# Moving the final residual tasks and weight sums of a two-layer mixer kernel into one half of its second block, and reordering the first block's background tasks

## The chip, the cores and the metric

The kernel runs on one core of one Trainium2 chip. The metric is device time in microseconds (us), the median of several runs. Profiles are of one execution. The engines are named as in the profile: PE (TensorE, matmuls), PEld (its weight loads), DVE (VectorE), ACT (ScalarE), POOL (GpSimd) and SP (SyncE); SPq is SP's queue, from which most loads are issued, and POOL issues the stores.

## What is computed

Two layers over a residual stream x of 2048 tokens by 1024 channels, all in fp32:

```python
for l in range(DEPTH):                                   # 2 layers
    mod = silu(c) @ w_ada[l] + b_ada[l]                  # conditioning: shift, scale, gate
    shift, scale, gate = jnp.split(mod, 3, axis=-1)
    h = rms_norm(x, g_pre[l]) * (1.0 + scale) + shift
    proj = h @ w_in[l]                                   # 1024 -> 3072
    # u_a, b_a, c_a, gate_a, u_p, gate_p: 512 columns each
    y_a = b_a * causal_conv3(c_a * u_a, w_conv[l]) * silu(gate_a)
    y_p = pool(u_p, w_pool[l], pool_scale[l]) * silu(gate_p)
    y = jnp.concatenate([y_a, y_p], axis=-1) @ w_out[l]  # 1024 -> 1024
    x = x + gate * rms_norm(y, g_post[l])
```

`pool` takes causal means over 2, 4, 8 and 16 tokens, less the token itself, and mixes each group of 128 channels with a 128 x 128 matrix. Every fp32 matmul is made of three products of high and low parts.

## The kernel before

**Blocks.** There are four blocks: layer 0 tokens 0 to 1023, layer 0 tokens 1024 to 2047, then the same for layer 1. A block has an input stage (the product with `w_in`, with the convolution and pooling behind it) and an output stage (the product with `w_out`, `out_phase`), in which the operands of the next block's input stage are made as well. The first block's input stage is plain (`in_phase`): for a pair of 512-token halves, 24 groups of 128 columns, each 8 turns; a turn is one 128-channel slice, three passes over two halves, six matmuls (line 395, the same line as in the output stage). The third and fourth block multiply three groups of a kind at a time with seven products instead of eight (`in_seven`, line 868), from weight sums that were computed earlier and stored in DRAM (`sums`). The second block is mixed: its first twelve column groups are done plainly (`in_phase` with `some` given, 96 turns, here called the **plain half**), its last six pairs by `in_seven` (the **sevenths half**, 42 products of 12 matmuls, which makes its own sums from the raw weights on DVE, lines 758 to 765).

**Background tasks.** Work that belongs to other blocks is cut into tasks with a load part and a list of steps with an estimated cost in us. `Paced` runs them between the turns: it spreads the estimated total evenly over a given number of turns (in the plain half over 72 of its 96, so that all are done some 10 turns before its end), holds at most two tasks open (`abreast=2`), and asks for the load of the next task when a task is begun (`lead` 1). The order in which the code calls the engines is the order of each engine's queue (`manual_schedule`): a queue does nothing behind an instruction that waits. The tasks that matter here:

- `mix_task`: two parts of a layer-one pooling weight; loads `wupt` (line 415), four small PE matmuls (line 421), stores `wu`.
- fills (`fill` in `out_phase`): load `late` (line 1123), cast on ACT, subtract on DVE (line 1134); operands of the sevenths half.
- `finish_tasks`, the **final tasks**, 16 of them: load `ysp` (line 1180) and x (line 1181), DVE multiply (1184) and add (1186), POOL store to `x1` (1191), ACT square (1197), DVE sum (1200). After the eighth of each half `stat_steps` splits the sum on ACT and DVE (368, 370), and five turns later PE forms the mean (313).
- `sum_task`, the **weight sums** of layer one: four loads of 128 KB (456), four DVE operations (464 to 467), ACT casts (470, 472), DVE subtractions (474, 476), four POOL stores of 256 KB (478, 479, two at 481).
- `x_stat_task` and `x_stat_end`: squares of the first layer's x for the second block, and their mean.
- `ada_task`: conditioning, two loads and two DVE operations (263, 267) a task; 8 for layer zero's gate and 16 for layer one's scale and shift.

**Buffers.** Loads of tasks land in `landing` tiles of 128 x 512, four in the first block and five in the second; the build gives a new tile the buffer that the program freed first, and the load then waits for that buffer's last reader or store. In the second block a final task takes two, a sum two, a fill and a mix one each. The final task's second tile (x) is the one that is stored, so it is free when the store has landed; the first is free after the square's sum (line 1200). Sums in the first block land in wide tiles of another pool.

**Weights.** In the plain stages `Weights` loads a half of a column group (line 202, SP) 16 turns before PE uses it, casts it on ACT (211) and forms the low part on DVE (221) six turns before.

Of the kernel before, what the change touches and what calls it, by code (L numbers as in the profile page):

```python
# [16 lines left out]
KT = D // P  # L17
# [4 lines left out]
NH = TB // HS  # L22
# [11 lines left out]
def trunk(ctx: ExitStack, tc: tile.TileContext, xt, c, wada, vec, rcp, win, wupt, wpool, wout, out):  # L34
# [210 lines left out]
    def ada_fin(l, kind, k0, k1):  # L245
        s = slice(kind * KT + k0, kind * KT + k1)
        ks = slice(k0, k1)
        nc.vector.tensor_tensor(mod[:, l, s], mod[:, l, s], mod2[:, l, s], op=ALU.add)
        nc.vector.tensor_tensor(mod[:, l, s], mod[:, l, s], vecs[:, l, V_ADA + s.start : V_ADA + s.stop], op=ALU.add)
        if kind == 1:  # L250
            nc.vector.scalar_tensor_tensor(
                apre[:, l, ks], mod[:, l, s], 1.0, vecs[:, l, V_PRE + k0 : V_PRE + k1], op0=ALU.add, op1=ALU.mult
            )
        elif kind == 2:
            nc.vector.tensor_tensor(gg[:, l, ks], mod[:, l, s], vecs[:, l, V_POST + k0 : V_POST + k1], op=ALU.mult)

    def ada_task(l, j):
        w = []

        def load():  # L260
            for n in range(2):
                w.append(landing("adaw"))
                nc.sync.dma_start(w[n], wada[l, j][:, n * HS : (n + 1) * HS])

        def steps():
            for n, m in enumerate((mod, mod2)):
                nc.vector.scalar_tensor_tensor(  # L267
                    w[n], w[n], 1.0, cb[:, n * HS : (n + 1) * HS], op0=ALU.mult, op1=ALU.mult, accum_out=m[:, l, j : j + 1]
                )
                yield E2  # L270

        return load, steps, 2 * E2

    def call_task(f, us):
        def steps():
            f()
            yield us

        return (lambda: None), steps, us
# [1183 lines left out]
    def between(many, few):  # L1463

        r, n = [], len(few)
        for i, t in enumerate(many):
            r.append(t)
            r += few[i * n // len(many) : (i + 1) * n // len(many)]
        return r

    with working(9, 4, 4, 3, 0):
        with tc.manual_schedule(engines={E.DVE, E.PE, E.Activation}):
            hrhs, started = start(0)
        with tc.manual_schedule():
            later = Later()
            accs = {}
            tasks = [mix_task(0, g, n, later) for g in range(1, NCG) for n in range(2)]
            rest = [ada_task(0, 2 * KT + k) for k in range(KT)]
            rest += [call_task(lambda: ada_fin(0, 2, 0, KT), 0.3)]
            rest += [ada_task(1, j) for j in list(range(8, 16)) + list(range(8))]  # L1480
            rest += [call_task(lambda: (ada_fin(1, 1, 0, KT), ada_fin(1, 0, 0, KT)), 0.5)]
            rest += [x_stat_task(1, s, k, accs) for s in range(NH) for k in range(KT)]
            tasks += between(rest, [sum_task(1, n, u, True) for n, u in mine("AB")])
            tasks += [x_stat_end(1, s, accs, later) for s in range(NH)]
            tasks += [call_task(lambda: load_wpool(1), 0.1)]
            ws = out_weights(0, turned(wplaces, 34))
            y = in_phase(0, 0, hrhs, tasks, later, started, yplaces, wplaces, ws)
# [39 lines left out]
    with working(5, 6, 5, 6, 2), tc.manual_schedule():  # L1527
        plain = [(kind, i) for kind, i in IN_ORDER if i < PLAIN]
        pairs = [(kind, i) for kind, i in PAIRS if i >= PLAIN]
        first = in_weights(0, plain, 0, turned(ws.places, 16))  # L1530
        h, fills, opening, hrhs = out_phase(0, 0, y, 0, 1, ws, hplaces, yorder, first, True)
        ring = first.places + hplaces[8 : 8 + KH]
        wts = Sevenths(0, ring, pairs, True)
        later = Later()
        mixes = [mix_task(1, g, n, later) for g in range(NCG) for n in range(2)]
        fins = finish_tasks(0, 0, later)
        sums_ = [sum_task(1, n, u, False) for n, u in mine("P")]
        cut = 6
        tasks = between(fills, mixes) + between(fins[:cut], sums_[:3])
        in_phase(0, 1, hrhs, tasks, later, None, None, first.places, wts, first, opening, plain)  # L1540
        hp = {}
        for k in range(KH):
            hp["B11", k], hp["B21", k], hp["B22", k] = hplaces[k], hplaces[KH + k], hplaces[12 + k]
        it = iter(yorder)
        for name in ("T2", "T3", "T1", "T4"):
            for k in range(KH):
                hp[name, k] = next(it)
        ws, closing, done = block_end(0, 1, hp, ring, pairs, False, (3, 2, 3, 2, 2, 2))
        kept = in_seven(0, 1, h, [], None, between(fins[cut:], sums_[3:]), later, wts, closing, pairs)
        y, yorder, wplaces, hplaces, _ = done(kept)  # L1550
    with working(5, 8, 6, 3, 2), tc.manual_schedule():
        for n, (l, b) in enumerate(blocks[2:], 2):
            lplaces = yorder[4:]
            ring = wplaces[1:] + yorder[:4] + wplaces[:1]
            wts = Sevenths(l, ring, PAIRS)
# [62 lines left out]
```

## Time and profile before

| | us |
|---|---|
| median of 3 runs | 1437.48 (1436.09 to 1438.05) |
| the profiled execution | 1435.26, span 1433.5 |
| PE busy | 1379.6 (96%), 6178 matmuls |
| DVE busy | 982.8 (69%) |
| ACT / POOL busy | 522.6 / 227.0 |
| DMA | 306.97 MB, mean 214 GB/s |

The profile gives busy time by engine, by group of instructions (line, engine, operation, tiles, count, mean duration, idle time before it and what ended it), the chain of work that ended last, who waited for whom, and a timeline. Times of instructions are us from the span's start. PE is busy 96% of the span, so what can be won or lost lies in the few stretches where it isn't dense.

### The profile page before, as it was taken

Reading aid. Unit: us, or ns where it says so; the run is one execution under the profiler, and the core shown is the slowest. Engines: PE = TensorE matmul, PEld = TensorE weight load, DVE = VectorE, ACT = ScalarE, POOL = GpSimd, SP = SyncE. Lnnn points to the kernel's source line nnn. Section 1 sums busy time; section 2 is a strip of 40 time slices with the busy share of each in tenths; the row PEclk is TensorE's granted clock in tenths of the full one; section 3 lists DMA queues with packets and bytes.
Section 4 is the critical chain, followed back from the end, with each engine's and each line's share of the span. In section 5 each row is a group of like instructions: output and inputs, shape, how many; then the busy total and the mean of one; then the engine's idle time right before and its main releaser. Section 6 shows DMA issues by size and latency. Waiting matters only on the chain.

```text
span 1433.5 us, 17996 instructions
## 1 busy us (share of the span) xinstructions
PE 1379.6 (96%) x6178; PEld 1126.0 (79%) x6178; DVE 982.8 (69%) x1645; ACT 522.6 (36%) x905; POOL 227.0 (16%) x365
## 2 busy tenths in 40 slices
PE   8999999989999999796999999999999999999996
PEld 4778888878888888565688888888888888888796
DVE  7765988956645568688775767768766755657555
ACT  5332324445643323232755321213656211112421
POOL 0001213211100111111022121221112122221000
PEclk9999999999999999998999999999999999999998
DMA  8416888855627563455567888797559777877422
GB/s 318 176 45 224 282 308 289 299 191 175 236 91 239 186 219 125 177 169 187 183 238 256 265 264 251 228 284 238 194 201 302 211 237 229 255 224 239 154 89 88
DMA packets 149598, 306.97 MB, mean 214 GB/s; under 512 B 16641, under 2 KB 33025, under 8 KB 149506
## 3 DMA queue, kind: packets, MB, share of 16 engines
q1 hardware_dynamic: 100658, 179.44, 38.2%
q0 software_dynamic: 48848, 126.38, 26.3%
q8 instruction: 48, 0.79, 0.2%
q14 instruction: 44, 0.36, 0.1%
HBM read 225.54 MB, written 80.22 MB: 213 GB/s over the span
## 4 chain that ended last, share of the span: by engine, by line
PE 73%; issue 9%; DVE 9%; DMA 5%; ACT 2%; POOL 1%; SPq 1%; DVEq 0%; ACTq 0%; POOLq 0%
PE ps_in L868 31%; PE ps_out L395 23%; PE ps_in L395 17%; DMA raw<-win 1%; PE ps_wu L421 1%; DMA sums<-raw 1%; DMA raw<-wout 1%; DVE y L188 1%; DVE ws L221 1%; DVE win L497 1%; DMA fin<-xt 0%; PE ps_warm L1304 0%; DVE adaw L267 0%; PE ps_stat L1321 0%; DMA xin<-xt 0%
## 5 line engine op out<-in xcount | busy, mean ns | idle before, releaser
L868 PE MATMUL ps_in<-h,ws 128*128 128x512 f32 x2520 | 583.8, 392 | 24.1 <-ACT ws L777 13.2
L868 PEld LDWEIGHTS ps_in<-h,ws 128*128 128x128 f32 x2520 | 473.5, 189 | 133.0 <-ACT ws L777 16.9
L395 PE MATMUL ps_out<-y,ws 128*128 128x512 f32 (+1 forms) x1728 | 355.6, 367 | 5.1 <-ACT ws L211 2.1
L395 PEld LDWEIGHTS ps_out<-y,ws 128*128 128x128 f32 x1728 | 298.0, 189 | 62.2 <-ACT ws L211 3.9
L395 PE MATMUL ps_in<-h,ws 128*128 128x512 f32 x1392 | 321.3, 391 | 0.0
L395 PEld LDWEIGHTS ps_in<-h,ws 128*128 128x128 f32 x1392 | 261.4, 189 | 54.1
L211 ACT CAST ws<-raw 128x512 fp32r<-128x512 f32 x122 | 74.7, 621 | 192.2 <-PE ps_in L395 73.0
L221 DVE TENSOR_TENSOR ws<-raw,ws 128x512 fp32r<-128x512 f32 x122 | 83.2, 687 | 83.2 <-ACT ws L211 83.2
L777 ACT CAST ws<-raw 128x512 fp32r<-128x512 f32 x108 | 65.3, 618 | 170.7 <-DMA raw<-win 49.0
L740 POOL DMA_DIRECT2D ws<-sums x96 | 67.6, 705 | 207.4 <-PE ps_in L868 178.7
L395 PE MATMUL ps_in<-h,w 128*128 128x512 f32 x336 | 81.1, 400 | 5.6 <-DVE h L387 2.8
L395 PEld LDWEIGHTS ps_in<-h,w 128*128 128x128 f32 x336 | 63.2, 190 | 22.6 <-DVE h L387 3.6
L787 DVE TENSOR_TENSOR ws<-raw,ws 128x512 fp32r<-128x512 f32 x108 | 73.9, 685 | 7.3 <-ACT ws L777 7.1
L1067 POOL DMA_DIRECT2D ysp<-yg x48 | 26.1, 545 | 217.6 <-ACT yg L1066 217.0
L267 DVE SCALAR_TENSOR_TENSOR adaw<-adaw,cb 128x512 f32<-128x512 f32 x64 | 42.5, 686 | 15.6 <-PE ps_wu L421 9.2
L912 ACT ACTIVATE second<-second 128x1024 f32<-128x1024 f32 x20 | 21.2, 1062 | 85.5 <-DVE second L906 82.6
L891 ACT COPY v<-ps_in 128x512 f32<-128x512 f32 x30 | 17.6, 585 | 83.2 <-PE ps_in L868 83.2
L1186 DVE TENSOR_TENSOR fin<-fin 128x512 f32<-128x512 f32 x48 | 32.9, 685 | 20.1 <-DMA fin<-xt 20.0
L1075 DVE TENSOR_TENSOR acc<-acc,sq 128x512 f32<-128x512 f32 x42 | 28.6, 690 | 21.2 <-ACT sq L1072 21.1
L906 DVE TENSOR_TENSOR second<-ps_in,v 128x512 f32<-128x512 f32 x20 | 13.8, 688 | 41.3 <-PE ps_in L868 41.3
L1066 ACT ACTIVATE yg<-ps_out,gg 128x512 f32<-128x512 f32 x48 | 33.0, 689 | 14.7 <-PE ps_out L395 14.7
L478 POOL DMA_DIRECT2D sums<-s13h x24 | 17.3, 719 | 129.6 <-ACT s13h L470 108.1
(191 smaller groups left out, 1341.4 us busy)
## 6 DMA issues: line engine op xcount, KB each, us to landing
ws<-sums POOLq DMA_DIRECT2D x96, 512.0 KB, 7.3
raw<-win SPq DMA_DIRECT2D x122, 256.0 KB, 4.9
adaw<-wada SPq DMA_DIRECT2D x64, 256.0 KB, 4.9
raw<-wout SPq DMA_DIRECT2D x64, 256.0 KB, 4.7
sums<-raw POOLq DMA_DIRECT2D x48, 256.0 KB, 4.9
ysp<-yg POOLq DMA_DIRECT2D x48, 256.0 KB, 3.5
fin<-ysp SPq DMA_DIRECT2D x48, 256.0 KB, 5.0
yraw<-yin SPq DMA_DIRECT2D x42, 256.0 KB, 4.1
```

Source lines behind the costliest of these rows:

```text
L211: nc.scalar.copy(self.ws[m][:, 0], self.raws[m].rearrange("p (a b) -> p a b", b=P))
L221: nc.vector.tensor_tensor(t[:, 1], raw, t[:, 0].bitcast(F32), op=ALU.subtract)
L267: nc.vector.scalar_tensor_tensor(w[n], w[n], 1.0, cb[:, n * HS : (n + 1) * HS], op0=ALU.mult, op1=ALU.mult, accum_out=m[:, l, j : j + 1])
L395: nc.tensor.matmul(ps[s], lhsT=ws[k // KH][:, wi, k % KH, :], rhs=rhs(k, ri, s), start=first and (wi, ri) == PASSES[0], stop=last and (wi, ...
L740: nc.gpsimd.dma_start(t.rearrange("p a b c -> p a (b c)"), sums[self.l, PAIRS.index((kind, i))][:, :, SUM[a]])
L777: nc.scalar.copy(self.place(m)[:, 0], self.raws[m].rearrange("p (a b) -> p a b", b=P))
L787: nc.vector.tensor_tensor(t[:, 1], raw, t[:, 0].bitcast(F32), op=ALU.subtract)
L868: nc.tensor.matmul(ps, lhsT=ops[m][:, wi, k, :], rhs=h[hn][k][:, ri, :], start=p < 4 and k == 0 and (wi, ri) == (0, 0), stop=k == KH - 1 a ...
L1066: nc.scalar.activation(t, ps[s], AF.Copy, scale=gg[:, l, j : j + 1])
L1067: nc.gpsimd.dma_start(ysp[l, b][:, j, s * HS : (s + 1) * HS], t)
L1075: tt(accs[s], accs[s], q, op=ALU.add)
L1186: nc.vector.tensor_tensor(e[1], e[1], e[0], op=ALU.add)
```

## The change

In the second block, all 16 final tasks and all 8 sums of kind P go to the tasks of the plain half; `in_seven` gets none. In the first block, the statistics of x come first (mixed with the gate's conditioning and ten of the sixteen sums), their end follows, and layer one's conditioning comes last with the other six sums.

```diff
             tasks = [mix_task(0, g, n, later) for g in range(1, NCG) for n in range(2)]
-            rest = [ada_task(0, 2 * KT + k) for k in range(KT)]
-            rest += [call_task(lambda: ada_fin(0, 2, 0, KT), 0.3)]
-            rest += [ada_task(1, j) for j in list(range(8, 16)) + list(range(8))]
-            rest += [call_task(lambda: (ada_fin(1, 1, 0, KT), ada_fin(1, 0, 0, KT)), 0.5)]
-            rest += [x_stat_task(1, s, k, accs) for s in range(NH) for k in range(KT)]
-            tasks += between(rest, [sum_task(1, n, u, True) for n, u in mine("AB")])
+            rest = [x_stat_task(1, s, k, accs) for s in range(NH) for k in range(KT)]
+            made = [sum_task(1, n, u, True) for n, u in mine("AB")]
+            tasks += between(between(rest, [ada_task(0, 2 * KT + k) for k in range(KT)]), made[:10])
+            tasks += [call_task(lambda: ada_fin(0, 2, 0, KT), 0.3)]
             tasks += [x_stat_end(1, s, accs, later) for s in range(NH)]
+            tasks += between([ada_task(1, j) for j in list(range(8, 16)) + list(range(8))], made[10:])
+            tasks += [call_task(lambda: (ada_fin(1, 1, 0, KT), ada_fin(1, 0, 0, KT)), 0.5)]
...
         sums_ = [sum_task(1, n, u, False) for n, u in mine("P")]
-        cut = 6
-        tasks = between(fills, mixes) + between(fins[:cut], sums_[:3])
+        tasks = between(fills, mixes) + between(fins, sums_)
         in_phase(0, 1, hrhs, tasks, later, None, None, first.places, wts, first, opening, plain)
...
-        kept = in_seven(0, 1, h, [], None, between(fins[cut:], sums_[3:]), later, wts, closing, pairs)
+        kept = in_seven(0, 1, h, [], None, [], later, wts, closing, pairs)
```

SP's queue in the plain half, second block, before. `fin` are the two tiles of a final task, `raw0`/`raw1` those of a sum, `raw` a weight of the plain half; behind "waits" stand the semaphores (DMAHW: a load's, DMASW: a store's):

```order
L1180 DMA fin_4058<-ysp0_0_131 128x512 [waits DMAHW7_49,DMASW1_49,Activation_49]
L1181 DMA fin_4059<-xt 128x512 [waits DMAHW0_49,DMASW3_49,Activation_49]
L202 DMA raw_4082<-win 128x512 [waits DMAHW1_49]
L1180 DMA fin_4102<-ysp0_0_131 128x512 [waits DMAHW2_49,DVE_49]
L1181 DMA fin_4103<-xt 128x512 [waits DMAHW3_49,DMASW6_49,DVE_49]
L202 DMA raw_4123<-win 128x512 [waits DMAHW4_49]
L202 DMA raw_4163<-win 128x512 [waits DMAHW5_49]
L456 DMA raw0_4166<-win 128x256 [waits DMAHW6_49,DMASW7_49,DVE_49]
```

And after, in the same half:

```order
L1180 DMA fin_4000<-ysp0_0_131 128x512 [waits DMAHW4_49,DMASW7_49,DMASW4_49]
L1181 DMA fin_4001<-xt 128x512 [waits DMAHW5_49,DMASW0_49,Activation_49]
L202 DMA raw_4026<-wu0_1_89 128x512 [waits DMAHW6_49]
L1180 DMA fin_4048<-ysp0_0_131 128x512 [waits DMAHW7_49,DVE_49]
L1181 DMA fin_4049<-xt 128x512 [waits DMAHW0_49,DVE_49]
L456 DMA raw0_4069<-win 128x256 [waits DMAHW1_49,DMASW1_49]
L456 DMA raw0_4069<-wu1_1_93 128x256 [waits DMAHW2_49]
L456 DMA raw1_4072<-win 128x256 [waits DMAHW3_49,DMASW4_49]
L456 DMA raw1_4072<-wu1_1_93 128x256 [waits DMAHW4_49]
L202 DMA raw_4084<-wu0_1_89 128x512 [waits DMAHW5_49]
L1180 DMA fin_4096<-ysp0_0_131 128x512 [waits DMAHW6_49,DMASW5_49]
L1181 DMA fin_4097<-xt 128x512 [waits DMAHW7_49,DMASW6_49,Activation_49]
```

Fewer weight loads (line 202, one every four turns) now stand between the tasks' loads: two final tasks and a sum follow each other within about seven turns, where it was thirteen to fifteen.

DVE's queue in the same place, before (`ws` is a low part of a weight that PE uses six turns later):

```order
L221 TENSOR_TENSOR ws_4121<-raw_4035,ws_4121 128x512 [waits DMAHW6_49,Activation_49]
L1186 TENSOR_TENSOR fin_4059<-fin_4059,fin_4058 128x512 [waits DMAHW0_49,DMASW3_49,DVE_49]
L1184 TENSOR_TENSOR fin_4102<-fin_4102,ry_3523 128x512 [waits DMAHW2_49]
L221 TENSOR_TENSOR ws_4161<-raw_4082,ws_4161 128x512 [waits DMAHW1_49,Activation_49]
L1186 TENSOR_TENSOR fin_4103<-fin_4103,fin_4102 128x512 [waits DMAHW3_49,DMASW6_49,DVE_49]
```

And after:

```order
L221 TENSOR_TENSOR ws_4082<-raw_3956,ws_4082 128x512 [waits Activation_49]
L1186 TENSOR_TENSOR fin_4049<-fin_4049,fin_4048 128x512 [waits DMAHW0_49,DVE_49]
L464 TENSOR_TENSOR s13_4100<-raw0_4069,raw1_4072 128x256 [waits DMAHW3_49,DMAHW1_49,DMASW5_49]
L465 TENSOR_TENSOR s13_4100<-raw0_4069 128x256 [waits DMAHW2_49]
L466 TENSOR_TENSOR raw0_4069<-s13_4100,raw0_4069 128x256 [waits DMASW1_49,DVE_49]
L467 TENSOR_TENSOR raw1_4072<-raw1_4072,raw0_4069 128x256 [waits DMAHW4_49,DMASW4_49,DVE_49]
L1200 TENSOR_TENSOR xacc_3905<-xacc_3905,fin_4048 128x512 [waits Activation_49]
L1184 TENSOR_TENSOR fin_4096<-fin_4096,ry_3523 128x512 [waits DMAHW6_49,DMASW5_49]
L1186 TENSOR_TENSOR fin_4097<-fin_4097,fin_4096 128x512 [waits DMAHW7_49,DMASW6_49,DVE_49]
L221 TENSOR_TENSOR ws_4127<-raw_4026,ws_4127 128x512 [waits Activation_49]
```

Between two weights' low parts now stand the additions of two final tasks and a sum's operations, where there was one addition.

PE's queue over the first block's end (`ps_stat` is a mean of squares, `ps_in` the input stage), as a difference of before (-) and after (+):

```order
-L395 MATMUL ps_in<-h,ws 128x512 x750
-L313 MATMUL ps_stat<-ah,ones 128x512
-L313 MATMUL ps_stat<-al,ones 128x512
-L395 MATMUL ps_in<-h,ws 128x512 x6
-L313 MATMUL ps_stat<-ah,ones 128x512
-L313 MATMUL ps_stat<-al,ones 128x512
-L395 MATMUL ps_in<-h,ws 128x512 x30
+L395 MATMUL ps_in<-h,ws 128x512 x438
```

After that row the two pairs of `ps_stat` follow, twelve matmuls apart, and 336 matmuls more to the block's end: the statistics stand in the middle of the block instead of at its end.

## Rows read from the trace of the kernel before

**Rows 1.** Chain that ended last, in time: start, us, what; third block.

```profile
790.42 117.01 PE ps_in L868 x516
```

**Rows 2.** Busy time by stretch: engines' us (instructions), clock, DMA share, GB/s.

```profile
398.20:537.00 138.80, 138.80 (x646) 115.88 (x645) 75.64 (x121) 50.44 (x92) 18.82 (x31) 1.00 0.56 188
537.00:687.70 150.70, 125.70 (x509) 95.89 (x507) 120.43 (x197) 47.44 (x90) 21.80 (x34) 0.95 0.50 166
687.70:708.30 20.60, 18.51 (x77) 13.81 (x77) 15.49 (x25) 15.83 (x22) 0.00 (x0) 1.00 0.57 190
790.00:907.00 117.00, 117.00 (x517) 96.85 (x516) 83.39 (x140) 29.77 (x48) 25.38 (x39) 1.00 0.82 256
```

**Rows 3.** Waits of PE, 537 to 710: who for whom, us in total, times, longest.

```profile
PE ps_in L868 <- ACT ws L777: 13.2, 9, 5.3
PE ps_in L868 <- ACT fin L1197: 8.0, 1, 8.0
PE ps_in L868 <- DVE ws L787: 2.8, 7, 0.7
```

**Rows 4.** Timeline of PE, 270 to 330, the first block's end.

```profile
296.38 0.50 PE L313 MATMUL ps_stat<-al,ones 128*128 128x512 f32 x1 [0.40 <-DVE al L370]
...
301.55 0.51 PE L313 MATMUL ps_stat<-ah,ones 128*128 128x512 f32 x1 [3.27 <-ACT ah L368]
```

**Rows 5.** DVE's groups, 537 to 687.7: count, busy us, mean ns, idle before.

```profile
L1186 DVE TENSOR_TENSOR fin<-fin 128x512 f32<-128x512 f32 x10 | 6.9, 690 | 18.8 <-DMA fin<-xt 18.7
...
L476 DVE TENSOR_TENSOR raw<-raw 128x256 fp32r<-128x256 f32 x10 | 3.8, 417 | 0.0
...
L474 DVE TENSOR_TENSOR s<-s,s13h 128x512 fp32r<-128x512 f32 x5 | 3.4, 680 | 0.0
...
L466 DVE TENSOR_TENSOR raw<-s,raw 128x256 f32<-128x256 f32 x5 | 2.1, 426 | 0.2
```

**Rows 6.** Waits of SP's queue, 470 to 537: us in total, times, longest.

```profile
SPq L1181 <- DMA sums<-raw: 20.6, 3, 8.4
SPq L1181 <- DMA x<-fin: 7.1, 2, 4.3
```

**Rows 7.** Timeline of SP's queue, 474 to 510: second loads of final tasks.

```profile
478.78 0.33 SPq L1181 DMA_DIRECT2D fin<-xt  x1
...
486.45 0.33 SPq L1181 DMA_DIRECT2D fin<-xt  x1
...
508.68 0.33 SPq L1181 DMA_DIRECT2D fin<-xt  x1
```

**Rows 8.** Timeline of DVE, 483 to 520.

```profile
490.38 0.69 DVE L1186 TENSOR_TENSOR fin<-fin 128x512 f32<-128x512 f32 x1 [0.77 <-DMA fin<-xt]
...
499.58 0.42 DVE L464 TENSOR_TENSOR s<-raw,raw 128x256 f32<-128x256 f32 x1
...
512.00 0.69 DVE L1186 TENSOR_TENSOR fin<-fin 128x512 f32<-128x512 f32 x1 [0.49 <-DMA fin<-xt]
```

**Rows 9.** Timeline of POOL, 466 to 530: stores of a final task and of a sum.

```profile
475.59 0.54 POOL L1191 DMA_DIRECT2D x<-fin  x1
...
491.37 0.54 POOL L1191 DMA_DIRECT2D x<-fin  x1 [5.74 <-DVE fin L1186]
```

**Rows 10.** Timeline of DVE, 541 to 545 (541.22) and 617 to 620 (618.43).

```profile
541.22 0.69 DVE L1186 TENSOR_TENSOR fin<-fin 128x512 f32<-128x512 f32 x1
...
618.43 0.69 DVE L1186 TENSOR_TENSOR fin<-fin 128x512 f32<-128x512 f32 x1
```

**Rows 11.** Timelines of SP's queue (419.69) and PE (427.14): a mix's load and use.

```profile
419.69 0.33 SPq L415 DMA_DIRECT2D wupt<-wupt  x1
...
427.14 1.05 PE L421 MATMUL ps_wu<-wp,wupt 128*128 128x128 f32 x8
```

**Rows 12.** Busy time by stretch, columns as in rows 2.

```profile
200.00:220.00 20.00, 20.00 (x90) 16.57 (x89) 19.69 (x46) 5.88 (x12) 3.57 (x5) 1.00 0.78 262
300.00:320.00 20.00, 18.23 (x72) 14.75 (x73) 9.47 (x14) 9.14 (x15) 0.00 (x0) 0.91 0.56 186
```

## The prediction

> **What bounds the kernel now.** I read the busy shares first, then TensorE (PE) stage by stage, then the queues behind the stage that loses. PE is dense nearly everywhere: in the third block 516 matmuls take 117.01 us, 226.8 ns each [rows 1]. That is the yardstick. The second block falls into two parts. Its plain half (576 matmuls with eight small weight mixes) runs from 398.2 to 537.0 with PE busy all 138.8 us. Its sevenths half needs 504 x 226.8 ns = 114.3 us and takes 150.7 [rows 2]: 36.4 us lost, 0.9 of it for two pairs of statistics matmuls. The next stage loses 3.4 us more before it is dense: 76 matmuls are 17.2 us of its first 20.6 [rows 2]. In the half PE waits for weights that ScalarE and VectorE (DVE) hand over late, 16.0 us behind lines 777 and 787, and once 8.0 behind ScalarE's square of a final task [rows 3]; the mean clock of 0.95 [rows 2] takes another 7.5 us (0.05 x 150.7). So what the sevenths half holds up is real and lies on the critical path. The first block loses a little at its end: PE waits 0.40 and 3.27 us for the statistics of x [rows 4], and at a mean clock of 0.91 (part of the stretch at 1.2 GHz, after those waits [rows 12]) the 20 us from 300 lose 1.8.
>
> **What the change takes out.** Ten final tasks and five weight sums leave the sevenths half. On DVE the ten additions of final tasks are 6.9 us, the multiplications as many of the same size, nine sums of squares and two splits of 0.69 us 7.6; the sums' operations are 3.4 + 3.8 + 4 x 2.1 [rows 5]. That is 37.0 us of 120.4 busy; DVE also stood still there for 18.8 us before the second addition of a final task, waiting for its load [rows 5]. With 83.4 us left (some 90 with what ran over the half's end) in 114 us nothing there is short any more: the third block runs dense with 83.4 DVE us in 117 [rows 2]. I take the half at 114.3 + 1 for its closing, which is a gain of 35.4, and 3.4 for the start of the output stage. First block: the statistics' matmuls now stand 336 matmuls ahead of the block's end instead of 30, and only five turns behind the DVE subtraction that they need, as before; I keep 1 us of wait there and take 4.5 of the 5.5 as gained. The conditioning of layer two, now last, is read only two stages later, and its loads are as many as before, so I cost that move at nothing; the bound is the same 3.7 us of waits, if a last sum held something up instead. Gains: 35.4 + 3.4 + 4.5 = 43.3 us.
>
> **What it costs in the plain half.** By busy time there is room: DVE 75.6 of 138.8 us [rows 2], with 37.0 more 81%. But the tasks don't flow by busy time. They live in the five landing buffers: a final task takes two of them, a sum two, and in the order of before and after a final task's second load (line 1181) reuses a buffer of the final task before it, of whose store it has to see the end, or of a sum. I read that in the trace: between 470 and 537 SP stands 20.6 + 7.1 us at line 1181, for stores of sums and stores of x1 [rows 6], while only six final tasks and three sums are under way. One link of this chain, from rows: load issued at 486.45, addition at 490.38 [rows 7, 8], 3.9 us (508.68 to 512.00 gives 3.3); addition 0.69 us; then the store, whose issue ends at 475.59 + 0.54 = 476.13 and which lets SP's waiting load go at 478.78 [rows 7, 9], 2.7 us after, with 0.3 + 0.54 before it (addition's end 491.07, issue 491.37 to 491.91). Together 3.6 + 0.7 + 3.5 = 7.8 us. Of the fifteen links in the new order (a buffer goes to the next load that finds it freed first) eight go through the store of a final task; two through a sum's stores, which take 9.1 us (four operations from 499.58, SP released at 508.68 [rows 7, 8]) and with load and addition some 13; four through the square and an addition only, some 5; the first is free, some 2. That is (8 x 7.8 + 2 x 13 + 4 x 5 + 2) / 15 = 7.4 us; the first loads, the sums' own operations and DVE's foreground work come in between, and I take 7.8. The shortest I can make of the rows is 3.3 + 0.7 + 3.1 = 7.1; the longest is the pace at which the tasks really went where they were crowded, the sevenths half: the second additions of seven final tasks in a row start from 541.22 to 618.43, six intervals of 12.9 us [rows 10], but there DVE was late for its own work too. I use 9.5 as the upper end.
>
> Against that, the program asks for much more. The plain half's pacing now has sixteen final tasks and eight sums to place in turns 33 to 86 (a turn is six matmuls, 1.36 us): first to last final task 47 turns, 64 us, 4.3 us a link. Before, it was 33 turns for five links, 9 us each, and the chain kept up. So the chain falls behind by 15 x (7.8 - 4.3) = 53 us. DVE takes its queue in order, and the low parts of PE's weights (line 221) stand between those additions: in the order, one of them stands behind two second loads. PE uses such a low part six turns, 8.2 us, after its place in the order; that is the slack it has. (The weights' loads on SP, line 202, stand behind line 1181 too, but sixteen turns ahead of their use.) Three more small terms. Fills and mixes are crowded too, into 16 turns instead of 27, through the same five buffers; PE came to a mix's operand 7.4 us after the issue of its load in the closest case (419.69 to 427.14) [rows 11]; the new order puts some loads behind fills that are just being used, and I estimate 6 us of waits over the eight mixes (0 to 10). Behind the last final task come the rest of the last sum and a weight: about 1.5 us more than before. One stretch at 1.2 GHz in the broken-up half, as there were two in the sevenths half: 1.7 us (0 to 7.5, what the sevenths half loses by its clock). The sum: 53 - 8.2 + 6 + 1.5 + 1.7 = 54 us.
>
> Net: 54 - 43.3 = 10.7 us slower. The profiled execution took 1435.26 us (span 1433.5), 2.2 under the median of 1437.48; 1437.5 + 10.7 = 1448.
>
> **A rule that speaks against this.** The row first: DVE is 80% busy in the sevenths half (120.43 of 150.7) and 54% in the plain one [rows 2]. The Trainium skill, "Perfetto Trace Analysis", section Optimization Strategy, tells one to find the most-contended engine by its occupancy and to interleave stretches in which different engines are contended; by that rule the move is right, and nothing but the gains would be left. The same section says that a gap that repeats can mean that there are too few buffers for the next tile; SP's stops in rows 6 are that, and they are in the half that is to take the work. I follow the second.
>
> **The rivals.** (A) Buffers don't hold; DVE's and PE's time do. DVE with 81% in the plain half is less than the first block had in 200 to 220 (19.69 of 20 us, PE dense [rows 12]). Then the gains stand alone, less the mixes' 6 us: 1437.5 - 43.3 + 6 = 1400. Against it: the stops of rows 6. Chance 0.08. (B) The chain holds but is quicker, since links through DVE alone outnumber what I think or stores land in less: it decides at a link of 7.1 us. There the chain is 42 us late, the half 43 longer, and the end is 1437.5 + 43 - 43.3 = 1437; at 6.5 it is 1428. It is not slower than before by anything that shows. For it: the 2.7 us of the store were at a busy time. Against: DMA will be busier (0.56 now [rows 2]; ten tasks with three transfers of a 128 x 512 tile and five sums with six tiles' worth are 15.7 MB more, in 139 us 113 GB/s on 188). Chance 0.22: 0.10 under 1434.6, 0.10 within 0.2% of now, 0.02 above. (C) The forecast, links from 7.3 to 8.9 us: 1440.5 to 1464. Chance 0.60. (D) Links of 9 us and more, since the sums' four stores and the weights' own traffic lengthen each, or further stretches at 1.2 GHz: at 9.5 us the chain is 25 us later than in the forecast, 1473. Chance 0.10.
>
> **How the numbers follow.** The likeliest case gives 1448. About 0.2% (2.9 us) is what a measurement of this kernel tells from no change. Faster: 0.08 + 0.10 = 0.18; within: 0.10; slower: 0.72. The range leaves out A and the quick end of B (0.12) and what of D is above 1466 (0.08): 1428 to 1466.
>
> **What would show each step.** In the changed kernel's profile: the sevenths half dense, 504 matmuls in about 115 us, no wait at line 868; the plain half 180 to 195 us long instead of 139, with PE waits at line 395 behind DVE's line 221 and, at the statistics, behind line 370; DVE idle before line 1186 for a load of x, in sum above 30 us; SP at line 1181 for most of the time from 455 on; second loads of consecutive final tasks about 8 us apart; no wait of 3.3 us before the statistics at the end of the first block. It is wrong if the plain half stays under 160 us: then links are shorter than any row shows, or DVE's order leaves PE more slack than six turns. If the sevenths half still loses 10 us or more, the loss there was not the moved tasks' but its own weights'.

## The result, and the profile of the changed kernel

The changed kernel takes 1452.61 us (median, 1451.67 to 1453.75) against 1437.67 of the kernel before on the same chip: a ratio of 1.0106, 95% interval 1.0089 to 1.0124. It is slower by 15 us, where 10.7 were forecast. Its profiled execution has a span of 1451.0 us (1433.5 before).

By stretches: plain half, sevenths half, start of the output stage (length; busy us and instructions of each engine; TensorE's mean granted clock, DMA's share, GB/s). The fourth row is the part of the plain half in which the tasks are crowded. They answer to rows 2.

```profile
core 0: us, PE busy (x) PEld busy (x) DVE busy (x) ACT busy (x) POOL busy (x), PEclk, DMA share, GB/s
398.70:593.00 194.30, 155.07 (x650) 124.40 (x649) 109.53 (x187) 63.59 (x119) 38.85 (x61) 0.90 0.62 207
593.00:707.40 114.40, 114.40 (x506) 94.75 (x505) 89.33 (x133) 36.95 (x65) 2.17 (x4) 1.00 0.29 95
707.40:728.00 20.60, 19.34 (x82) 14.88 (x82) 15.49 (x24) 14.59 (x21) 0.00 (x0) 1.00 0.52 170
480.00:593.00 113.00, 79.89 (x289) 62.03 (x290) 68.05 (x121) 28.52 (x57) 27.62 (x42) 0.84 0.66 224
```

The sevenths half is dense: 114.4 us instead of 150.7 [rows 2]. The plain half is 194.3 us long instead of 138.9 (398.04 to 536.99 before). What TensorE waits for there (us in total, times, longest), where it waited for nothing before:

```profile
PE ps_in L395 <- DVE ws L221: 28.0, 6, 7.1
PE ps_in L395 <- ACT ws L211: 4.2, 1, 4.2
PE ps_wu L421 <- DMA wupt<-wupt: 3.1, 2, 1.6
PE ps_stat L313 <- ACT ah L368: 2.8, 1, 2.8
PE ps_stat L313 <- DVE al L370: 1.1, 1, 1.1
```

These are 39.2 of the 55.4 us by which the half is longer. The other 16 are in TensorE's busy time: 155.07 us, instead of 138.96 (dense) before, for the same matmuls and four more, those of the final tasks' statistics (0.9 us). So some 15 us are the clock, by this difference: its mean is 0.84 in the 113 us from 480 (a part of them at 1.2 GHz), 1.00 in the whole half before [rows 2]. How one of these waits comes about is seen on VectorE (DVE) from 490 to 504, each row with the idle time ahead of it and what ended that:

```profile
492.64 0.69 DVE L1186 TENSOR_TENSOR fin<-fin 128x512 f32<-128x512 f32 x1 [3.55 <-DMA fin<-xt]
495.65 0.42 DVE L464 TENSOR_TENSOR s<-raw,raw 128x256 f32<-128x256 f32 x1 [2.32 <-DMA raw<-win]
...
498.82 0.69 DVE L1184 TENSOR_TENSOR fin<-fin,ry 128x512 f32<-128x512 f32 x1 [0.68 <-DMA fin<-ysp]
501.57 0.69 DVE L1186 TENSOR_TENSOR fin<-fin 128x512 f32<-128x512 f32 x1 [2.05 <-DMA fin<-xt]
502.18 0.69 DVE L221 TENSOR_TENSOR ws<-raw,ws 128x512 fp32r<-128x512 f32 x1
```

In these rows VectorE stands four times for loads of tasks, 8.6 us of the 13 up to 502.2, and the low part of a weight (line 221) comes behind them. TensorE was waiting for it and starts when it is done. Its rows (idle time ahead in brackets) also show what follows a wait:

```profile
483.10 12.71 PE L395 MATMUL ps_in<-h,ws 128*128 128x512 f32 x48 [6.13 <-DVE ws L221]
502.92 7.50 PE L395 MATMUL ps_in<-h,ws 128*128 128x512 f32 x24 [7.11 <-DVE ws L221]
```

The 48 matmuls after the wait of 6.13 us take 265 ns each, the 24 after that of 7.11 us 312, not the 226.8 of rows 1; the mean granted clock is 0.88 from 483.10 to 495.81 and 0.75 from 502.92 to 510.42. Behind VectorE stands SP, in whose queue the loads wait for buffers (SP's waits, 440 to 600), and the sixteen second loads of final tasks run from 452.1 to 570.5, 118.4 / 15 = 7.89 us apart:

```profile
SPq L1181 <- DMA x<-fin: 26.8, 7, 6.0
SPq L456 <- DMA sums<-raw: 17.3, 5, 5.2
SPq L1181 <- DMA sums<-raw: 16.2, 2, 11.1
...
SPq L456 <- DVE xacc L1200: 6.9, 2, 3.7
SPq L1180 <- DMA x<-fin: 6.7, 2, 4.1
```

```profile
L1181 SPq DMA_DIRECT2D fin<-xt x16: 327/330/415, 452.1 to 570.5; - x16
```

Could the stop reach TensorE by another way, by the weights' own loads (line 202), which stand behind line 1181 in SP's queue? In this trace no cast and no low part waits for such a load. VectorE's waits from 440 to 593:

```profile
DVE fin L1186 <- DMA fin<-xt: 31.7, 10, 7.1
...
DVE ws L221 <- ACT ws L211: 2.2, 1, 2.2
```

So the way to the weights is VectorE's order. The one wait for ScalarE's cast (4.2 us) has the same root: that cast stands behind a final task's square, for which ScalarE waited 3.05 us for VectorE.

The first block brings little. The second block begins at 398.68, before at 398.04, 0.6 us later. But the start of this execution is 2.2 us longer: the 22 matmuls that TensorE begins at 66.66 before begin at 68.86 here. The start varies whatever the order of the tasks: the same matmuls begin at 66.75 in the run fins below, which has the new order, and at 68.80 in b_l7, which has the old one. From them to the second block it is 329.8 us instead of 331.4; over the traces here 326.4 to 331.9 in nine with the new order (mean 329.8), 330.5 to 332.3 in three with the old (mean 331.4). Of the 4.5 us forecast some 1.6 came.

### The profile page after: what moved, and what is told of

Its sections match the earlier page's. It is cut to its first block, busy times and chain, and to the rows that moved or that the text cites. A ratio compares the mean times of both kernels' runs of the same rounds, so it can differ in the third digit from the quotient of the medians.

```text
span 1451.0 us, 18013 instructions
## 1 busy us (share of the span) xinstructions
PE 1385.0 (95%) x6178; PEld 1134.8 (78%) x6178; DVE 984.0 (68%) x1645; ACT 523.8 (36%) x905; POOL 227.9 (16%) x365
## 4 chain that ended last, share of the span: by engine, by line
PE 74%; DVE 8%; issue 8%; DMA 7%; ACT 2%; POOL 1%; SPq 1%; DVEq 0%; POOLq 0%; ACTq 0%
PE ps_in L868 37%; PE ps_out L395 22%; PE ps_in L395 13%; DMA raw<-win 2%; DMA late<-late 1%; DVE ws L221 1%; DMA fin<-xt 1%; DVE y L188 1%; DMA adaw<-wada 1%; DMA raw<-wout 1%; DMA ws<-sums 1%; PE ps_stat L1321 0%; PE ps_warm L1304 0%; DVE win L497 0%; PE ps_wu L421 0%
## 5 line engine op out<-in xcount | busy, mean ns | idle before, releaser
L1186 DVE TENSOR_TENSOR fin<-fin 128x512 f32<-128x512 f32 x48 | 32.9, 686 | 31.8 <-DMA fin<-xt 31.7
L1197 ACT ACTIVATE fin<-fin 128x512 f32<-128x512 f32 x28 | 17.7, 631 | 92.8 <-DVE fin L1186 63.9
L267 DVE SCALAR_TENSOR_TENSOR adaw<-adaw,cb 128x512 f32<-128x512 f32 x64 | 42.7, 686 | 12.3 <-DMA adaw<-wada 12.3
L1066 ACT ACTIVATE yg<-ps_out,gg 128x512 f32<-128x512 f32 x48 | 33.1, 689 | 13.8 <-PE ps_out L395 13.7
```

What stands on the lines that cost most here:

```text
L267: nc.vector.scalar_tensor_tensor(w[n], w[n], 1.0, cb[:, n * HS : (n + 1) * HS], op0=ALU.mult, op1=ALU.mult, accum_out=m[:, l, j : j + 1])
L1066: nc.scalar.activation(t, ps[s], AF.Copy, scale=gg[:, l, j : j + 1])
L1186: nc.vector.tensor_tensor(e[1], e[1], e[0], op=ALU.add)
```

## The experiments

Ratios are to the kernel before, timed on the same chip beside each run.

**The two parts apart.** p_second has only the second block's edit, p_first only the first block's.

> Only the second block's part of the change; the first block's tasks in the order of before. Theory that the chain of landing buffers costs the plain half 55 us and that the first block's new order gained about 1 us (in the trace of after the wait at the statistics has moved from 301.5 to 233.5, 2.9 instead of 3.3 us, and the stretch at 1.2 GHz from 312.7 to 244.1): 1452 to 1456 us, the plain half near 194 us long, the sevenths half near 114. Rival, the prediction's own term for the first block (4.5 us gained by the new order and lost again to something else): 1457 us and over.

> Only the first block's part of the change; the second block as before. If the wait at the statistics only moves: 1435 to 1438 us, within 0.2% of before, with one wait of about 3 us at the first statistics pair's successor in the middle of the block and none at its end. The prediction's term (4.5 us gained) would give 1433.

Measured: p_second 1449.77 us, ratio 1.0099 (1.0076 to 1.0122); p_first 1436.26, 1.0003 (0.9988 to 1.0019). The whole slowdown is the second block's part. p_second lies a little below both theories' numbers, but the kernel before was 2.4 us quicker beside it, too (1435.25, against 1437.67 beside the changed kernel). The first block's part is worth nothing that can be measured in times: a gain of 1.7 us at most by the interval. The reason stands in the trace of the changed kernel, on VectorE and on TensorE:

```profile
229.66 0.69 DVE L267 SCALAR_TENSOR_TENSOR adaw<-adaw,cb 128x512 f32<-128x512 f32 x1 [3.44 <-DMA adaw<-wada]
...
232.79 0.68 DVE L370 TENSOR_TENSOR al<-acc,ah 128x512 fp32r<-128x512 f32 x1
```

```profile
233.53 0.77 PE L313 MATMUL ps_stat<-al,ones 128*128 128x512 f32 x1 [2.91 <-DVE al L370]
```

And on SP:

```profile
213.36 11.34 SPq L202 DMA_DIRECT2D raw<-win  x3
224.75 6.67 SPq L263 DMA_DIRECT2D adaw<-wada  x6
```

The second low part of the statistics now stands behind a conditioning operation of layer two whose load is late, since SP had stood at the weights' loads (line 202, three issues over 11.34 us from 213.36) before it issued it. In p_first's profiled execution, the fastest of its ten (1432.15), the same wait was 0.95 us and the first block 326.4 us long, so the wait varies from one execution to the next.

**More and fewer landing buffers.** a_l7 has seven and a_l4 four instead of five; the order of the instructions is that of the changed kernel.

```diff
-    with working(5, 6, 5, 6, 2), tc.manual_schedule():
+    with working(5, 6, 7, 6, 0), tc.manual_schedule():
...
-                    v = held["v"].tile([P, HS], F32, tag="v", name="v")
+                    v = held["v"].tile([P, HS], F32, tag="v", name="v") if "v" in held else landing("v")
```

(a_l4: only the third number, 4.)

> The kernel after with seven landing buffers instead of five in the second block (the two that the sevenths half held for itself are taken from the same pool, since no task is left there); every engine's instructions stand in the same order. If the chain through the landing buffers sets the plain half, a load waits for a buffer freed seven tiles earlier instead of five: a link shrinks from 7.9 us towards 7.9 x 5/7 = 5.6, the chain is 15 x 2.3 = 34 us shorter, the plain half 150 to 170 us long instead of 194, the time 1412 to 1430 us. If DVE's or SP's occupancy by the added tasks sets it, buffers change nothing: 194 us and 1452.

> The kernel after with four landing buffers instead of five in the second block. By the chain of buffers a link grows from 7.9 us towards 7.9 x 5/4 = 9.9 us, 15 x 2 = 30 us more: the plain half 215 to 230 us long, 1475 to 1490 us in all. If occupancy sets the half: no change, 1452.

Measured: a_l7 1418.5 us, 0.9885 (0.9848 to 0.9923); a_l4 1479.78, 1.0307 (1.0273 to 1.0341). Both as the chain of buffers has it; occupancy would have given 1452 twice. The second loads in a_l4, then in a_l7 (the columns before the semicolon: shortest, median and longest issue in ns, first and last start):

```profile
L1181 SPq DMA_DIRECT2D fin<-xt x16: 328/328/382, 456.0 to 599.8; - x16
```

```profile
L1181 SPq DMA_DIRECT2D fin<-xt x16: 327/330/412, 446.3 to 536.0; - x16
```

That is 9.59 us a link with four buffers, 7.89 with five, 5.98 with seven. Times the buffers: 38.4, 39.5 and 41.9 us, nearly one number. The plain half follows: 219.7, 194.3, and in a_l7 159.3, with VectorE nearly as busy (108.75 us) as in the changed kernel (109.53) and the DMA engines moving more (253 GB/s instead of 207), so neither of them sets the pace:

```profile
399.60:558.90 159.30, 146.12 (x649) 119.38 (x648) 108.75 (x187) 63.78 (x119) 38.66 (x61) 0.97 0.73 253
```

**The final tasks' arithmetic on GpSimd.**

```diff
-                nc.vector.tensor_tensor(e[0], e[0], ry[l, b, s], op=ALU.mult)
+                eng = nc.gpsimd if (l, b) == (0, 0) else nc.vector
+                eng.tensor_tensor(e[0], e[0], ry[l, b, s], op=ALU.mult)
...
+                eng.tensor_tensor(e[1], e[1], e[0], op=ALU.add)
```

(and the sum of squares alike.)

> The kernel after (five landing buffers) with the final tasks' multiplication, addition and sum of squares (lines 1184, 1186, 1200) in the second block's plain half on GpSimd instead of VectorE. If the slow chain reaches TensorE only because VectorE takes its queue in order and stands at line 1186 in front of the weights' low parts (line 221), the tasks may stay about 8 us apart, but TensorE waits little: the plain half near 139 to 160 us, 1400 to 1425 us in all. If it reaches TensorE by another way (SP's weight loads behind line 1181, or the buffers themselves), the plain half stays near 194 us, 1452. No run here has shown GpSimd do such an operation; over some 5 us each would lengthen every link and bring the waits back.

Measured: 1458.5 us, 1.0151 (1.0131 to 1.0170); plain half 202.2. This is neither of the two times expected, and it doesn't decide what it was meant to. The weight sums' operations were left on VectorE, and it now stands for their loads; on GpSimd the operations take twice as long and lengthen the links to (579.4 - 450.7) / 15 = 8.58 us. VectorE's longest wait, then two groups on GpSimd (busy us, mean ns, idle before):

```profile
DVE s L464 <- DMA raw<-win: 59.0, 8, 11.0
```

```profile
L1185 POOL TENSOR_TENSOR fin<-fin,ry 128x512 f32<-128x512 f32 x16 | 23.8, 1490 | 7.1 <-DMA fin<-ysp 7.0
L1187 POOL TENSOR_TENSOR fin<-fin 128x512 f32<-128x512 f32 x16 | 22.0, 1378 | 17.0 <-DMA fin<-xt 16.6
```

**The store taken out of the landing buffer.**

```diff
-                nc.vector.tensor_tensor(e[1], e[1], e[0], op=ALU.add)
+                xo = half("xo") if (l, b) == (0, 0) else e[1]
+                nc.vector.tensor_tensor(xo, e[1], e[0], op=ALU.add)
+                e[1] = xo
```

> The kernel after (five landing buffers, all tasks in the plain half), but the final tasks' addition (line 1186) writes its result into one of the six half buffers instead of the landing buffer of x, and the store and the square read it there. The landing buffer then comes free at the end of the addition and not at the end of the store. If the store is the long part of a link (3.5 of 7.8 us by rows 7 to 9), the links through a store shrink to about 4.3 to 5 us, and the mean of fifteen to 5.6: the chain is 15 x (7.9 - 5.6) = 34 us shorter, the plain half 150 to 170 us, the time 1412 to 1432. If the loads' own landing or the sums' stores carry the chain, or the half buffers now fill up behind the stores, links stay over 7 us and the time over 1440.

Measured: 1438.42 us, 1.0016 (1.0000 to 1.0032); plain half 182.1, links (556.8 - 451.2) / 15 = 7.04 us. The gain is there, but a third of what was expected. The half buffers didn't fill up; VectorE waited for one three times, 4.1 us in all. The store is not the long part of a link: five buffers x 7.04 us are 35.2, only 4.3 less than 39.5, not far from the 3.5 for which one store holds one buffer. So a link looks like no path of load, addition and store. It would be the time in which the pool gives out the three buffers that a final task and half a sum need: the sum of three holds, divided by five. One of the three got shorter.

**Only the final tasks in the plain half; the sums all in the sevenths half,** which tells the two readings apart.

```diff
-        tasks = between(fills, mixes) + between(fins, sums_)
+        tasks = between(fills, mixes) + fins
...
-        kept = in_seven(0, 1, h, [], None, [], later, wts, closing, pairs)
+        kept = in_seven(0, 1, h, [], None, sums_, later, wts, closing, pairs)
```

> Five landing buffers, all sixteen final tasks in the plain half, all eight weight sums in the sevenths half. Two theories of what a link is. As the prediction put it, a link is the path through one buffer, load, addition, store: then every link here goes through a store, 7.8 us, while the program leaves 45 turns, 61 us, for fifteen: 15 x (7.8 - 4.1) = 55 us late, the plain half near 185 us, the time 1445 or more. As the runs with four, five and seven buffers and the one with the result in a half buffer suggest, the pool is a store of places: a use holds a buffer some 13.2 us (7.89 us a link x 5 buffers / 3 uses), and a link takes its uses x 13.2 / buffers. Without sums that is 2 x 13.2 / 5 = 5.3 us: 15 x 1.2 = 18 us late less 8 of slack, the plain half 143 to 155 us. The sevenths half has 83 us of VectorE and some 25 of sums in 114 and loses 0 to 8 us. Time 1400 to 1420.

Measured: 1439.48 us, 1.0011 (0.9994 to 1.0029): the plain half is 141.5 us, the sevenths half 150.6.

```profile
397.90:539.40 141.50, 140.49 (x650) 116.68 (x649) 86.76 (x131) 53.97 (x95) 15.66 (x29) 1.00 0.61 207
539.40:690.00 150.60, 125.23 (x505) 98.05 (x503) 110.13 (x186) 44.40 (x87) 24.92 (x36) 0.92 0.43 146
```

```profile
L1181 SPq DMA_DIRECT2D fin<-xt x16: 327/328/648, 453.8 to 523.0; - x16
```

Of final tasks alone a link is (523.0 - 453.8) / 15 = 4.61 us, with five buffers and every store in its place. A path of 7.8 us for each link doesn't hold, though here too SP stands for stores of x1 in front of both loads of final tasks (17.5 + 9.0 us, 440 to 540). Two uses hold 5 x 4.61 = 23.1 us of buffer time; in the changed kernel a link held 39.5, so the one use of a sum holds some 16 us, by this difference. The changed kernel's trace gives the holds one by one, from the issue of a tile's load to what frees its buffer. SP and GpSimd, the first sum:

```profile
456.41 0.33 SPq L456 DMA_DIRECT2D raw<-win  x1
```

```profile
470.41 1.41 POOL L481 DMA_DIRECT2D sums<-raw  x2
```

Over its sixteen tiles a sum's tile takes 12.4 us from load to store on the mean, and the store lands 4.7 us after its issue (median): 17.1. The second tile of a final task takes 6.1 and 3.4: 9.5. The first tile, until the operation that reads it last (line 1200, or 1186 in the two tasks that have no line 1200), takes 13.7. The three are 40.3, an estimate from means and medians, for the 39.5 of the links. In this run the two of a final task are 12.5 + 10.6 = 23.1. So the tile with the store, on which the prediction built its path, is the one that is held shortest.

The other half was missed: the sums alone cost the sevenths half 36 us, as much as ten final tasks and five sums did before, with VectorE busy 110 of 150.6 us. SP's longest wait from 520 to 690, and then the chain at 625 to 631: SP, ScalarE, TensorE:

```profile
SPq L456 <- DMA sums<-raw: 81.2, 6, 18.3
```

```profile
625.04 0.33 SPq L456 DMA_DIRECT2D raw<-win  x1
...
625.88 0.43 SPq L729 DMA_DIRECT2D raw<-wu  x1
```

```profile
629.53 0.62 ACT L777 CAST ws<-raw 128x512 fp32r<-128x512 f32 x1 [13.16 <-DMA raw<-wu]
630.06 0.58 ACT L891 COPY v<-ps_in 128x512 f32<-128x512 f32 x1
```

```profile
630.69 11.36 PE L868 MATMUL ps_in<-h,ws 128*128 128x512 f32 x36 [9.60 <-ACT v L891]
```

SP stands 18.3 us in front of a sum's load, until an earlier sum's stores have landed. The half's own weight load (line 729) is queued behind it on SP. ScalarE takes its queue in order and stands for that weight in front of the copy that frees TensorE. In this run's sevenths half the short buffers reach TensorE through SP's queue, in the changed kernel's plain half through VectorE's.

**The division before, with seven buffers** (the kernel before with the edit of a_l7).

> The kernel before with the same seven buffers (the sevenths half's own two taken from the common pool). If the landing buffers are what held up the sevenths half too (VectorE stood 18.8 us before line 1186 there), some of its 36 us come back: 1415 to 1428. If it is VectorE's busy time there (80%), nothing changes: 1433 to 1438. The tile that was kept apart may now wait behind the tasks' buffers, which would make it slower.

Measured: 1414.92 us, 0.9852 (0.9835 to 0.9870), just under the range.

```profile
540.10:668.50 128.40, 118.48 (x510) 94.53 (x509) 120.92 (x198) 48.49 (x91) 21.79 (x34) 1.00 0.58 195
```

With the same work in the same order the sevenths half is 128.4 us instead of 150.7 [rows 2]. So 22 of the 36 us lost there were the buffers'. For the 14 that are left VectorE's time is the likely limit: it is busy 120.92 of 128.4 us, and the casts of weights on ScalarE, for which TensorE waits there, wait in their turn for VectorE's sums of raw weights and not for a load. No run takes VectorE's work alone away.

```profile
ACT ws L777 <- DVE raw L765: 45.7, 6, 9.8
```

**Other divisions.** Twelve final tasks in the plain half, with six sums and seven buffers (a_l7_c12), and with seven sums and five buffers (a_c12_7).

```diff
-        tasks = between(fills, mixes) + between(fins, sums_)
+        cut = 12
+        tasks = between(fills, mixes) + between(fins[:cut], sums_[:6])
...
-        kept = in_seven(0, 1, h, [], None, [], later, wts, closing, pairs)
+        kept = in_seven(0, 1, h, [], None, between(fins[cut:], sums_[6:]), later, wts, closing, pairs)
```

> Seven landing buffers, but only twelve of the sixteen final tasks and six of the eight sums in the plain half, the rest in the sevenths half. With links of 6.0 us (as the run with seven buffers showed) the eleven links in the plain half take 66 us, and the program leaves them the same stretch, 5.8 us each: the chain is no longer late, the plain half 139 to 146 us long instead of 159. The sevenths half gets 4 tasks and 2 sums back, some 15 us of VectorE on 83 of 114: if it stays dense, the time is 1402 to 1412; if these tasks' waits for loads stop VectorE there as before, it loses 5 to 12 us and the time is 1412 to 1420.

> Five landing buffers as in both kernels, but twelve final tasks and seven sums in the plain half and four and one in the sevenths half. By the chain: eleven links of 7.9 us are 87 us where the program leaves them about 54 turns, 73 us, so 14 us late less 8 of slack, with some 2 of clock: the plain half 143 to 155 us. The sevenths half has four tasks where it had ten and loses 0 to 10 us instead of 36. Time 1405 to 1422. If both halves are bound by VectorE's time, the loss only divides: about 1440.

Measured: a_l7_c12 1399.57 us, 0.9747 (0.9729 to 0.9764), just under the range; a_c12_7 1429.68, 0.9955 (0.9937 to 0.9973). With seven buffers both halves are dense, and in the second VectorE is busy 102.74 of 115 us without TensorE waiting:

```profile
397.00:538.00 141.00, 139.87 (x648) 116.30 (x647) 94.68 (x160) 58.59 (x108) 30.81 (x49) 1.00 0.72 249
538.00:653.00 115.00, 115.00 (x509) 95.22 (x508) 102.74 (x161) 41.80 (x76) 10.07 (x16) 1.00 0.42 141
```

With five the sevenths half is dense too (114.8 us), but the plain half is 170.7 us long, more than the 143 to 155 expected: twelve tasks and seven sums take 38 buffers, and the expectation had reckoned eleven paths of 7.9 us.

**The first block again.** a_l7_l12 sets the statistics' matmuls twelve turns behind what feeds them; c12i (on a_l7_c12) puts one conditioning column ahead of each end of the statistics.

```diff
-        later(5, mean)
+        later(12 if key[0] == 0 else 5, mean)
```

```diff
+            cond = [ada_task(1, j) for j in list(range(8, 16)) + list(range(8))]
+            ends = [x_stat_end(1, s, accs, later) for s in range(NH)]
+            tasks += [cond[0], ends[0], cond[1], ends[1]]
+            tasks += between(cond[2:], made[10:])
```

> Seven landing buffers, and the first block's two pairs of statistics matmuls 12 turns instead of 5 behind the operations that feed them. In the first block VectorE's second low part of the statistics (line 370) stands behind a conditioning addition (line 267) whose load comes 3.4 us late; TensorE meets it 2.9 to 3.4 us too early. If that wait and the stretch at 1.2 GHz after it are all that is lost there, they go: 3 to 6 us under the same kernel with 5 turns (1418.5), 1412 to 1416. If the wait moves again, no change.

> Seven landing buffers, twelve tasks and six sums in the plain half (1399.6 us), and in the first block the two ends of the statistics each behind one conditioning column of layer two, so that the loads of the conditioning are issued ahead of SP's stop at the weights (line 202) and VectorE's second low part (line 370) doesn't stand behind a late load. If the 3.0 us wait and the stretch at 1.2 GHz after it go: 1394 to 1397. If the wait moves to the weights' low parts, as with 12 turns, 1398 to 1400.

Measured: a_l7_l12 1417.24 us, 0.9873 (0.9851 to 0.9895), the same as a_l7. The waits at the statistics are gone, and others are there, for the low parts of weights. The first stands behind VectorE's stop of 3.45 us for a conditioning load; before the second VectorE works without a break from 271.4 on, after another such stop of 3.30 us:

```profile
231.15 6.20 PE L395 MATMUL ps_in<-h,ws 128*128 128x512 f32 x26 [1.55 <-DVE ws L221]
...
294.98 15.71 PE L395 MATMUL ps_in<-h,ws 128*128 128x512 f32 x68 [1.85 <-DVE ws L221]
```

c12i 1397.8 us, 0.9727 (0.9708 to 0.9747), the fastest kernel here, 38 us under the kernel before. Against a_l7_c12 it can't be told apart by these intervals; in the traces one wait of 1.73 us at the statistics is left of 3.02, and the second block begins at 395.24 instead of 397.01.

## Why the prediction was right, and where its steps were wrong

- **Sevenths half and output stage.** Right in size for the half: 36.3 us gained for 35.4 forecast. Of the 3.4 us at the start of the output stage 1.2 came: the first 76 matmuls, with a wait of 1.07 us for a low part behind them that is there before and after, take 19.4 us instead of 20.6. The reason given for the half was wrong in part. The prediction read VectorE's 80%, with 18.8 us of stops, as the limit of that half. b_l7 shows 22 of the 36 us to be the landing buffers' there too, and a_l7_c12 shows VectorE 89% busy (102.74 of 115) with TensorE dense. SP's stops for stores from 470 to 537 [rows 6] were read for the plain half; the same view of the sevenths half of the kernel before (537 to 690) has a longer one, and the prediction didn't look there:

```profile
SPq L1181 <- DMA sums<-raw: 47.4, 4, 14.6
```

- **First block: 4.5 us forecast, some 1.6 in the traces, nothing measurable in the times.** The step that failed is "I cost that move at nothing". It counted who reads the conditioning of layer two, and not who is queued behind its operations on VectorE: the second low part of the statistics. Bounding it by 3.7 us of waits was near the truth (2.9 us and a slower stretch after it).
- **Plain half: +54 forecast, +55.4 measured, out of other terms.** The chain less its slack was to be 44.8 us of waits for weights; they are 32.2, with 3.9 at the statistics. The clock was put at 1.7 us (0 to 7.5) and is some 15. That the sum came out is luck: one term is as much too large as the other is too small. Part of the one probably stands in for the other: while the tasks set the pace, a matmul at the lower clock fills time that TensorE would have waited. No run separates the two; in a_l7, with fewer waits, the mean clock is 0.97. Mixes: 3.1 us for 6.
- **Link: 7.8 us forecast, 7.89 measured, and yet no path of load, addition and store.** With final tasks alone it is 4.61 us, with the store elsewhere 7.04, and it goes with one over the number of buffers. That the forecast's mean came out right is luck. It counted only the stops at line 1181, and those it counted nearly right (eight behind a store of x1, two behind a sum's; 7 and 2 came). But SP also stood 24.2 us at the sums' loads (line 456) and 12.3 at the first loads of final tasks (line 1180): each of the three uses of a link can meet the late buffer. The long holders are the sums, some 17 us a buffer, and the prediction could have read that from SP's 20.6 us behind sums' stores against 7.1 behind x1's [rows 6]. The 3.1 us for a store in its shortest link stand in no row.
- **Rival A** (busy time alone, 1400) fell with a_l7: VectorE does the same work there in 35 us less. The Trainium skill, "Perfetto Trace Analysis", section Optimization Strategy, offered both readings (that the most-contended engine is found by occupancy stands in its section Identifying the Most-Contended Engine). Its sentence on gaps that repeat held: two more buffers took 35 us out of the plain half. Its sentence on interleaving, read as the prediction reads it, would have given the wrong sign with five buffers. With seven, spreading the work does pay: the division of a_l7_c12 is 15 us under that of b_l7 (1399.57 to 1414.92). B's condition, a shorter link, came with more buffers; D's longer link only with four.
- The signs named for the trace came: 114.4 us dense, 194.3 us, 31.7 us of VectorE's idle time before line 1186, second loads 7.9 us apart. The wait at the end of the first block went too, to the middle of it.
- **The net.** 10.7 us forecast, 15 measured. The two traces are 17.5 us apart (1451.0 and 1433.5). Against the forecast the first block is 5.1 us longer (2.2 of them the start), the start of the output stage 2.2 and the plain half 1.4; the sevenths half is 0.9 shorter, and 1.0 is gained later.

What stays open: how much VectorE's order costs by itself. The waits in the changed kernel's trace show it as the way by which the stop reaches TensorE in the plain half, but no run takes that way away: the one that was to do it left the sums on VectorE.

## What to carry to other kernels

A pool of buffers has a pace of its own: its number of buffers divided by what a task's uses hold, summed. Before work is moved to an engine that is less busy, that pace has to be compared with the pace of the program, and the use that holds longest (here the weight sums with four stores) matters more than the count of tasks. And of every moved operation that waits for a load one asks what is queued behind it, on its own engine and on the queue that issues the load: here two more buffers were worth 32 us (2.2%), and a move that looked free cost most of what it should have gained.

## What the runs showed of the chip that was not expected

GpSimd took 1.38 to 1.49 us for an operation on 128x512 elements that VectorE does in 0.69. And short waits went with a loss by the clock of two fifths of their own length: where TensorE stood nine times, 36 us from 477 to 593, its mean granted clock was 0.84 (a part of it at 1.2 GHz), some 15 us more. From 398.7 to 480, with 6 us of waits, it was 1.00.
